# A decoder layer with a gathered expert table: 96 instead of 64 tokens of the second tile by gather, up products of 288 instead of 320 columns

## The chip, the cores and the metric

The kernel runs on one core of one Trainium2 chip. The metric is device time in microseconds (us) of one execution; lower is better. The kernel before has a median of 1505.05 us in 3 runs (1504.67 to 1509.46). One execution was profiled. Every row below is from that execution, and times in rows count from its first instruction.

## The reference, cut to what matters

One decoder layer on 512 tokens of 1024 features: modulation, attention in two head groups, output projection, LayerNorm, and then PEER, an expert layer, followed by the last LayerNorm. The change touches PEER only:

```
q = (hx @ w_pq).reshape(128, 8, 2, 128)                 # per chunk of 128 tokens
sc = einsum('thpd,hpnd->thpn', q, sub_keys)
v_half, i_half = top_k(sc, 16)                           # 16 of 128 keys, two halves
top_s, top_pos = top_k(all 16 x 16 sums, 16)             # 16 of 256 pairs per head
idx = pair of keys -> expert number in 0..16383          # 8 heads x 16 = 128 experts a token
g = softmax(top_s)
a = gelu(einsum('thkd,td->thk', u_tab[idx], hx))         # "up" side
out = einsum('thk,thkd->td', g * a, v_tab[idx])          # "down" side
```

Each token picks 128 of 16384 experts. An expert is one row of 1024 f32 (4 KB) in `u_tab` and one in `v_tab`, 64 MB a table.

## The kernel before, in words

The 512 tokens are four tiles of 128. Up to about 361 us the kernel makes modulation, attention, output projection, LayerNorm and the scores of the keys. Then come two long stages, which the change touches.

**The up stage** (`u_block(e)`, e = 0 to 127, about 361 to 948 us). Block e holds 128 experts. Its 512 KB of `u_T` are loaded (`raw`, three buffers, L98), split by ScalarE into a rounded part `hi` (L90) and by VectorE into the rest `lo` (L91), and multiplied on TensorE with the tokens' features: eight k-slices, three products each (hi by hi, hi by low, low by hi; L114 to L116), so 24 products a block, each of TU columns, one per token. A gelu (L844) gives the activations. Blocks 32 to 111 store them to DRAM (`a_d`) from ScalarE's queue and load them again later (`a_b`); the others stay on chip. TU is 320: the tokens of tiles 2 and 3 and the last 64 of tile 1. This dense path computes every expert for each of its tokens.

**Gathers.** Tile 0 and the first HU = 64 tokens of tile 1 take another way on the up side. For them GpSimd issues indirect DMAs (`fetch`, L771) of 128 rows of `u_tab`, one row per partition, and VectorE multiplies the rows with the tokens' features `h2n` and sums (`dot`, L776). With tile 0 a gather serves one expert of each of 128 tokens, so its up side takes 128 gathers and dots. With 64 tokens a gather serves two experts of each token: the partitions 0 to 63 hold one, 64 to 127 the other, and `h2n` holds the 64 tokens twice. That takes 64 gathers and dots (`gather_part`). Its results go through a gelu, the half in the upper partitions is moved by a small DMA (`far`), and both multiply `g` of tile 1 (L793, L794). Five buffers `gb` hold gathered rows. Tile 0 also takes its down side by gather: 128 gathers of `v_tab`, each added by VectorE into `acc0` (L812).

**make_g.** While the up stage runs, VectorE, ScalarE and TensorE also build for tiles 2, 3 and then 1 the dense table of weights per expert and token (`oh`, `go`, `stage`; L710 to L723; 16 products of 128 columns a step, 48 steps) and write it to DRAM (`g_d`). Tile 1 waits until `gather_part` has set `weighted`. VectorE also runs the top-k of the tiles in the order 1, 2, 3, 0 (`topk`).

**The down stage** (`v_block(n)`, about 948 to 1481 us) multiplies per block of 128 experts the weights times activations with `v_blk`: 18 products of 512 columns for 384 tokens (tiles 1 to 3). The first HU columns of `w` are a copy of the weights (L918, ScalarE), since `g` of these tokens already holds the activations; the other TU are a product with `a` (L920, VectorE).

**Order.** The program interleaves these by generators with costs in us and a rate per block. `pull(gen, us)` advances a generator until the sum of its yields reaches the rate. A dot yields 1.25, an addition to `acc0` 1.2. The rates are RA for gathers before `weighted`, RB after it, RV in the down stage; top-k gets 2.6, 1.2 and at last 0.95 a block; `make_g` gets 0.56 steps a block (GRATE). At down block 116 all gathers that are left are pulled at once. Each engine runs its own instructions in the order fixed in the program, and the DMA queue of SyncE (SP) issues its transfers in order too.

## Time and profile before

| what | value |
|---|---|
| median of 3 runs | 1505.05 us (1504.67 to 1509.46) |
| profiled execution, its own time | 1506.13 us |
| its span, first to last instruction | 1504.4 us |
| mean granted TensorE clock | 0.983 |
| TensorE busy | 1419.4 us (94%) |
| VectorE busy | 1267.4 us (84%) |
| ScalarE busy | 827.4 us (55%) |
| GpSimd busy | 460.2 us (31%) |
| DMA moved | 446.18 MB, mean 297 GB/s |

Engine names in rows: PE is TensorE (PEld its weight loads), DVE VectorE, ACT ScalarE, POOL GpSimd, SP SyncE. Busy time of PE counts from the start of a product to its modelled end, and successive products overlap, so a stretch can show PE fully busy. DMA share is the time that all packets took, divided by 16 engines' time; since packets of one engine may overlap a little, it can pass 1.

### The profile page before, as it was taken

To read this page: it belongs to the slowest core of one execution; us is meant where nothing else is said; L and a number is where in the kernel's file an instruction comes from. 1 tells how busy PE (TensorE), PEld (TensorE's weight loads), DVE (VectorE), ACT (ScalarE), POOL (GpSimd) and SP (SyncE) were. 2 spreads that over 40 slices of the span, in tenths; PEclk is the share of its full clock that TensorE was granted. 3 is DMA by queue.
4 is the path that set the end of the run, shared out by engine and by line. 5 is a ranking of instruction groups with operands and counts; after the bars stand their busy time and mean duration, and the time that the engine had idled before them with its cause. 6 is when DMAs were issued, how large, how long until landed. Compare 5 with 4: busy or idle time off the path is not lost.

```text
span 1504.4 us, 22850 instructions
## 1 busy us (share of the span) xinstructions
PE 1419.4 (94%) x7837; PEld 1247.0 (83%) x7837; DVE 1267.4 (84%) x2602; ACT 827.4 (55%) x1523; POOL 460.2 (31%) x338
## 2 busy tenths in 40 slices
PE   6999988999889999899999999899999999999895
PEld 5777766888779999889999999788888888888684
DVE  6797776799999989779889877799898888997756
ACT  3466633334438998989999943344444444443341
POOL 0000000000254434275455555443443343443100
PEclk9999998999989999999999999999999999999998
DMA  8865453222598899799999999999999999999861
GB/s 301 290 214 165 158 196 133 85 85 71 185 327 290 300 317 348 262 342 411 405 379 403 409 415 395 362 338 347 351 350 368 384 382 384 377 383 391 302 202 56
DMA packets 181526, 446.18 MB, mean 297 GB/s; under 512 B 16609, under 2 KB 87649, under 8 KB 178210
## 3 DMA queue, kind: packets, MB, share of 16 engines
q1 hardware_dynamic: 123810, 263.83, 49.0%
q0 software_dynamic: 46080, 167.79, 29.8%
q10 hardware_dynamic: 11520, 13.11, 2.4%
q8 instruction: 61, 1.00, 0.3%
q14 instruction: 55, 0.45, 0.1%
HBM read 401.38 MB, written 43.26 MB: 296 GB/s over the span
## 4 chain that ended last, share of the span: by engine, by line
PE 59%; DVE 12%; DMA 11%; ACT 8%; issue 7%; POOL 3%; ACTq 0%; SPq 0%; DVEq 0%; POOLq 0%
PE acc L116 10%; PE acc L115 10%; PE acc L114 10%; PE bank L114 5%; PE bank L115 5%; PE bank L116 5%; DMA raw<-u_T 3%; ACT go L716 3%; DVE lo L91 3%; POOL gb L771 3%; PE st L116 3%; PE st L114 3%; PE st L115 3%; PE acc L720 2%; DMA raw<-v_blk 2%
## 5 line engine op out<-in xcount | busy, mean ns | idle before, releaser
L90 ACT CAST hi<-raw 128x1024 fp32r<-128x1024 f32 x288 | 301.7, 1051 | 460.0 <-PE acc L116 217.4
L91 DVE TENSOR_TENSOR lo<-raw,hi 128x1024 fp32r<-128x1024 f32 x288 | 351.6, 1222 | 123.3 <-ACT hi L90 119.7
L116 PE MATMUL st<-h2h,lo 128*128 128x320 f32 x1024 | 319.9, 314 | 14.3 <-DVE lo L91 14.0
L114 PE MATMUL st<-h2h,hi 128*128 128x320 f32 x1024 | 324.1, 317 | 9.6 <-ACT hi L90 9.6
L115 PE MATMUL st<-h2l,hi 128*128 128x320 f32 x1024 | 319.5, 312 | 0.0
L115 PE MATMUL acc<-lo,wh 128*128 128x512 f32 x756 | 295.5, 391 | 5.1 <-DVE lo L91 5.1
L114 PE MATMUL acc<-hi,wh 128*128 128x512 f32 x756 | 295.7, 391 | 3.2 <-ACT wh L928 2.9
L116 PE MATMUL acc<-hi,wl 128*128 128x512 f32 x756 | 296.0, 392 | 0.3 <-DVE wl L929 0.3
L771 POOL DMA_INDIRECT gb<-u_tab,ei x128 | 194.1, 1517 | 188.9 <-DVE gb L776 147.6
L776 DVE SCALAR_TENSOR_TENSOR gb<-gb,h2n 128x1024 f32<-128x1024 f32 x192 | 230.7, 1218 | 20.5 <-DMA gb<-u_tab,ei 15.7
L771 POOL DMA_INDIRECT gb<-v_tab,ei x128 | 158.6, 1239 | 247.6 <-DVE acc L812 225.7
L116 PEld LDWEIGHTS st<-h2h,lo 128*128 128x128 f32 x1024 | 194.4, 190 | 17.6 <-DVE lo L91 17.4
L114 PEld LDWEIGHTS st<-h2h,hi 128*128 128x128 f32 x1024 | 195.1, 190 | 11.9 <-ACT hi L90 11.9
L115 PEld LDWEIGHTS st<-h2l,hi 128*128 128x128 f32 x1024 | 195.0, 190 | 0.0
L771 POOL DMA_INDIRECT gb<-u_tab,eip x64 | 95.8, 1497 | 259.8 <-ACT hi L90 148.8
L716 ACT ACTIVATE go<-oh,iT 128x128 f32<-128x128 bf16 x384 | 168.2, 521 | 8.5 <-DVE oh L710 8.1
L115 PEld LDWEIGHTS acc<-lo,wh 128*128 128x128 f32 x756 | 142.7, 189 | 35.3 <-DVE lo L91 5.5
L114 PEld LDWEIGHTS acc<-hi,wh 128*128 128x128 f32 x756 | 142.8, 189 | 34.0 <-ACT wh L928 3.6
L116 PEld LDWEIGHTS acc<-hi,wl 128*128 128x128 f32 x756 | 142.6, 189 | 31.1 <-DVE wl L929 1.6
L812 DVE SCALAR_TENSOR_TENSOR acc<-gb,w,acc 128x1024 f32<-128x1024 f32 x127 | 162.6, 1281 | 1.0
L122 POOL TENSOR_TENSOR rs_r<-rs_v,mhalf 128x1 f32<-128x1 f32 (+1 forms) x12 | 11.0, 914 | 337.5 <-DVE rs_v L120 301.7
L720 PE MATMUL acc<-go,oh 128*128 128x128 f32 x768 | 108.4, 285 | 4.7 <-ACT go L716 4.7
(220 smaller groups left out, 2001.7 us busy)
## 6 DMA issues: line engine op xcount, KB each, us to landing
raw<-u_T SPq DMA_DIRECT2D x128, 512.0 KB
raw<-v_blk SPq DMA_DIRECT2D x128, 512.0 KB
wada<-w_adaT SPq DMA_DIRECT2D x48, 512.0 KB
g_d<-stage SPq DMA_DIRECT2D x24, 1024.0 KB
gl<-g_d SPq DMA_DIRECT2D x96, 256.0 KB
a_d<-a_s ACTq DMA_DIRECT2D x80, 160.0 KB
a_b<-a_d SPq DMA_DIRECT2D x80, 160.0 KB
raw<-w_pqT SPq DMA_DIRECT2D x16, 512.0 KB
```

What stands on the lines that cost most here:

```text
L90: split.hi = nc.scalar.copy(hi, src)
L91: split.last = nc.vector.tensor_sub(lo, src, hi.bitcast(F32))
L114: nc.tensor.matmul(ps, lh, rh, start=first, stop=False)
L115: nc.tensor.matmul(ps, lh, rl, start=False, stop=False)
L116: nc.tensor.matmul(ps, ll, rh, start=False, stop=last)
L122: nc.gpsimd.tensor_tensor(r, v, mhalf.to_broadcast([P, n]), op=OP.pow)
L716: nc.scalar.activation(go[:, i, :], oh0[:, :, i], AF.Copy, scale=iT[:, 2, t0 + i:t0 + i + 1])
L720: nc.tensor.matmul(ps[:, i * P:(i + 1) * P], oh1[:, 4 * u + i, :], go[:, 4 * u + i, :], start=True, stop=True)
L771: nc.gpsimd.indirect_dma_start(out=b, out_offset=None, in_=A[tab], in_offset=bass.IndirectOffsetOnAxis(ap=idx[:, j:j + 1], axis=0))
L776: paced(nc.vector.scalar_tensor_tensor(b, b, 1.0, h2n, op0=OP.mult, op1=OP.mult, accum_out=acc))
L812: paced(nc.vector.scalar_tensor_tensor(acc0, b, w0[:, j:j + 1], acc0, op0=OP.mult, op1=OP.add))
```

## The change

HU goes from 64 to 96, so TU goes from 320 to 288: 24 x 128 up products lose 32 columns each. `gather_part` becomes two passes. The first serves tokens 0 to 63 with two experts a gather (64 gathers and dots), the second tokens 64 to 95 with four experts a gather (32 gathers and dots; `h2n` holds 32 tokens four times). Each pass loads its list by small DMAs (`eip`, two and four), reloads `h2n` (two and four DMAs), takes its gelu, moves all its results by small DMAs into `far` (two and four), and multiplies `g` once. The rates RA, RV and the last top-k rate change: 1.6 to 2.0, 1.55 to 1.75, 0.95 to 0.8. RB and GRATE stay. The activations that are stored and loaded again have 288 columns instead of 320; the copy of weights in the down stage has 96 columns instead of 64 and the product there 288 instead of 320.

```diff
@@ -38,14 +38,14 @@
 GB = 8
 NS = 80
 GRATE = 0.56
-HU = 64
+HU = 96
 T0U = P + HU
 TU = S - T0U
 LAST = 4
 GBUF = 5
-RA = 1.6
+RA = 2.0
 RB = 1.9
-RV = 1.55
+RV = 1.75
 GP = 6
 AHEAD = 3
 FIN = 24
@@ -777,23 +777,25 @@
 
     def gather_part():
         ei = lists[1]
-        eip = gath.tile([P, HU], I32, name="eip")
-        nc.vector.tensor_copy(eip[0:HU], ei[0:HU, 0:HU])
-        dma(eip[HU:P], ei[0:HU, HU:P])
-        for r in range(2):
-            dma(h2n[r * HU:(r + 1) * HU], h2_d[1][0:HU])
-        dots = gath.tile([P, HU], F32, name="dots1")
-        for j in range(HU):
-            dot(fetch("u_tab", eip, j), dots[:, j:j + 1])
-            yield 1.25
-        nc.scalar.activation(dots, dots, AF.Gelu)
-        far = gath.tile([P, HU], F32, name="far")
-        dma(far[0:HU], dots[HU:P])
         g = best[1][1].rearrange("p h k -> p (h k)")
-        nc.vector.tensor_mul(g[0:HU, 0:HU], g[0:HU, 0:HU], dots[0:HU])
-        nc.vector.tensor_mul(g[0:HU, HU:P], g[0:HU, HU:P], far[0:HU])
+        for r0, n in ((0, 64), (64, 32)):
+            m = P // n
+            eip = gath.tile([P, n], I32, name=f"eip{r0}")
+            for q in range(m):
+                dma(eip[q * n:(q + 1) * n], ei[r0:r0 + n, q * n:(q + 1) * n])
+            for q in range(m):
+                dma(h2n[q * n:(q + 1) * n], h2_d[1][r0:r0 + n])
+            dots = gath.tile([P, n], F32, name=f"dots1{r0}")
+            for j in range(n):
+                dot(fetch("u_tab", eip, j), dots[:, j:j + 1])
+                yield 1.25
+            nc.scalar.activation(dots, dots, AF.Gelu)
+            far = gath.tile([P, P], F32, name="far", tag="far", bufs=1)
+            for q in range(m):
+                dma(far[r0:r0 + n, q * n:(q + 1) * n], dots[q * n:(q + 1) * n])
+            nc.vector.tensor_mul(g[r0:r0 + n], g[r0:r0 + n], far[r0:r0 + n])
+            yield 0.3
         weighted.append(True)
-        yield 0.3
 
     def gather_tile():
         ei = lists[0]
@@ -887,7 +889,7 @@
             g_piece(0, (e - NKEY + 2 * GP + 1) // 2)
         keep(e)
         if e < NB + NS:
-            budget[0] = pull(tk, budget[0] + (2.6 if 1 not in best else 1.2 if 2 not in best else 0.95))
+            budget[0] = pull(tk, budget[0] + (2.6 if 1 not in best else 1.2 if 2 not in best else 0.8))
         if 2 in best and e < NB + NS:
             c1 += GRATE
             while c1 >= 1.0:
```

## Rows read from the trace of the kernel before

**Rows 1.** The page: busy time, then DMA and GB/s in 40 slices.

```profile
PE 1419.4 (94%) x7837; PEld 1247.0 (83%) x7837; DVE 1267.4 (84%) x2602; ACT 827.4 (55%) x1523; POOL 460.2 (31%) x338
...
DMA  8865453222598899799999999999999999999861
GB/s 301 290 214 165 158 196 133 85 85 71 185 327 290 300 317 348 262 342 411 405 379 403 409 415 395 362 338 347 351 350 368 384 382 384 377 383 391 302 202 56
```

**Rows 2.** Windows: us; PE, PEld, DVE, ACT, POOL busy; PEclk; DMA share; GB/s.

```profile
388.70:681.70 293.00, 269.77 (x1783) 257.65 (x1783) 260.98 (x564) 227.52 (x385) 131.83 (x83) 0.97 0.86 306
450.00:600.00 150.00, 145.20 (x989) 138.71 (x988) 141.38 (x323) 133.85 (x231) 61.61 (x40) 1.00 0.88 314
681.70:867.40 185.70, 185.70 (x1358) 185.70 (x1357) 164.36 (x217) 174.11 (x316) 93.67 (x65) 1.00 1.02 402
867.40:947.70 80.30, 79.85 (x546) 79.23 (x546) 61.46 (x87) 32.41 (x48) 44.09 (x32) 1.00 1.03 403
947.70:1145.00 197.30, 193.03 (x848) 158.69 (x847) 174.06 (x228) 81.22 (x145) 81.89 (x64) 0.99 0.98 349
1145.00:1395.00 250.00, 250.00 (x1104) 207.09 (x1103) 218.23 (x257) 102.62 (x180) 96.04 (x78) 1.00 1.05 383
```

**Rows 3.** Timeline, PE, up block without make_g: first product and the next block's first.

```profile
879.72 0.31 PE L114 MATMUL st<-h2h,hi 128*128 128x320 f32 x1
...
883.24 0.31 PE L114 MATMUL st<-h2h,hi 128*128 128x320 f32 x1
```

**Rows 4.** Timeline, PE, down block: a product and the one 18 products later.

```profile
1200.10 0.39 PE L114 MATMUL acc<-hi,wh 128*128 128x512 f32 x1
...
1204.18 0.39 PE L114 MATMUL acc<-hi,wh 128*128 128x512 f32 x1
```

**Rows 5.** Timeline, one make_g step: 16 products of 128 columns on PE.

```profile
702.88 1.95 PE L720 MATMUL acc<-go,oh 128*128 128x128 f32 x16
```

**Rows 6.** The page, DMA queues: packets, MB, share of 16 engines' span.

```profile
q0 software_dynamic: 46080, 167.79, 29.8%
q10 hardware_dynamic: 11520, 13.11, 2.4%
```

**Rows 7.** Groups by line, VectorE, 388.7 to 681.7 us: busy, mean ns | idle before.

```profile
L776 DVE SCALAR_TENSOR_TENSOR gb<-gb,h2n 128x1024 f32<-128x1024 f32 x79 | 95.4, 1216 | 15.2 <-DMA gb<-u_tab,ei 10.9 <-DMA gb<-u_tab,eip 4.2
L91 DVE TENSOR_TENSOR lo<-raw,hi 128x1024 fp32r<-128x1024 f32 x58 | 70.5, 1217 | 7.1 <-ACT hi L90 7.1
```

**Rows 8.** Groups by line, TensorE, 388.7 to 681.7 us.

```profile
L114 PE MATMUL st<-h2h,hi 128*128 128x320 f32 x464 | 148.3, 320 | 9.1 <-ACT hi L90 9.1
L116 PE MATMUL st<-h2h,lo 128*128 128x320 f32 x465 | 146.0, 318 | 9.4 <-DVE lo L91 9.2
```

**Rows 9.** Waits of TensorE, 681.7 to 947.7 us: total, times, longest.

```profile
PE st L116 <- DVE lo L91: 0.3, 1, 0.3
```

**Rows 10.** Timeline of SP's queue where gather_part hands over to tile 0.

```profile
627.54 0.33 SPq L801 DMA_DIRECT2D h2n<-h_d  x1
638.85 0.33 SPq L726 DMA_DIRECT2D g_d<-stage  x1
...
643.33 16.09 SPq L98 DMA_DIRECT2D raw<-u_T  x6
```

**Rows 11.** Waits of SP's queue, whole span: total, times, longest.

```profile
SPq L726 <- ACT dots L789: 11.0, 1, 11.0
```

**Rows 12.** Groups by line, VectorE, 1145 to 1395 us.

```profile
L812 DVE SCALAR_TENSOR_TENSOR acc<-gb,w,acc 128x1024 f32<-128x1024 f32 x78 | 99.9, 1280 | 0.6
L91 DVE TENSOR_TENSOR lo<-raw,hi 128x1024 fp32r<-128x1024 f32 x60 | 73.4, 1223 | 29.9 <-ACT hi L90 28.2 <-issue 1.7
...
L920 DVE TENSOR_TENSOR w<-a_b,gl 128x320 f32<-128x320 f32 x59 | 28.6, 485 | 1.2 <-DMA a_b<-a_d 1.2
```

**Rows 13.** The copy of weights, L918: ns min/median/max, first and last start.

```profile
L918 ACT COPY w<-gl x128: 233/237/243, 947.1 to 1471.0; 128x64 f32<-128x64 f32 x128
```

## The prediction

> **What bounds the kernel now.** I read the page first: TensorE is busy 94% of the span, but its busy time counts modelled ends, so the number to look at is beside it, VectorE at 84%, and the two lines below, where the DMA digits stand at 9 from the middle of the up stage to the end of the gathers [rows 1]. Then the windows by stage [rows 2], since one answer doesn't hold for all of them.
>
> First half of the up stage, blocks 6 to 63 (388.7 to 681.7 us): TensorE needs less than it takes. A block of 24 products of 320 columns runs in 883.24 - 879.72 = 3.52 us, 146.7 ns a product [rows 3], and a make_g step of 16 products takes about 1.7 us (1.95 with the last one's tail, [rows 5]). The stretch has 1393 products of the first kind (those named L114 and L116 are in [rows 8], L115 has as many) and 24 steps: 1393 x 0.1467 + 24 x 1.7 = 204 + 41 = 245 us of 293. VectorE is busy 261 of 293, and in the middle of it 141.4 of 150, 94% [rows 2]; TensorE's waits that are seen are for what ScalarE and VectorE split [rows 8]. VectorE is the tightest here; DMA has room (share 0.86).
>
> Second half, blocks 64 to 127 (681.7 to 947.7): TensorE has no gap to speak of, 0.3 us of wait in 266 [rows 9], and DMA is full too: share 1.02 and 1.03, 402 and 403 GB/s [rows 2]. Two bounds lie on each other.
>
> Down stage: 18 products of 512 columns take 4.08 us, 226.7 ns each [rows 4], and TensorE is busy 250.00 of 250; the DMA share is 0.98 to 1145 us, then 1.05 at 383 GB/s with smaller packets [rows 2].
>
> **The products.** From 512 to 320 columns the pitch falls by 80 ns, 0.417 ns a column. So 288 columns give 133.3 ns, still above the 112 ns or so (1.95 us less some 0.27 of the last one's own, over 15) that products of 128 columns need [rows 5], and 32 columns are 13.3 ns: 3072 x 13.3 = 41.0 us of TensorE's work. By stretch: blocks 0 to 5 about 2 us, to block 63 18.6 us, after it 20.5 us (62.8 blocks or so at 0.32). The granted clock is 1.00 in nearly all windows, the upper level, 2.4 GHz [rows 2].
>
> The Trainium skill gives less: TensorE: Matmul & The Clock Gate, section Back-to-back issue gap, has a sustained spacing of 81 ns at 128 columns and 131 ns at 512, an estimate of 4.2 ns for 32 columns and 13 us in all. The 226.7 and 146.7 ns of this trace disagree with it, and the measurement decides.
>
> **The gathers.** I count them by the yields. The list of tile 1 is known at block 6. Before, 64 dots at 1.6 / 1.25 a block fill blocks 6 to 55, then 1.9 / 1.25 = 1.52 a block; in the down stage 1.55 / 1.25 and 1.55 / 1.2. After: 96 at 2.0 / 1.25 = 1.6 fill blocks 6 to 65, then 1.52, then 1.75 / 1.25 and 1.75 / 1.2 = 1.46. Up to block 63 that is 76 before (the trace has 79, [rows 7]) and 93 after; blocks 64 to 127 98 and 97; down stage 146 and 162, ending at down block 112 and 111. So 17 more in the first half, 1 less in the second, 16 more in the down stage. The weights of tile 1 are ready at block 66 instead of 55; make_g needs them at block 78, so nothing waits. Top-k of tile 0 ends at block 63 instead of 56, before the list is needed at 66.
>
> One gather is 29.8% x 1504.4 / 320 = 1.40 us of all DMA engines (0.52 MB); a store of activations 2.4% x 1504.4 / 80 = 0.45 us [rows 6], and a tenth of it, 0.045 us, falls away; I take the same for loading them. On VectorE one dot is 1.22 us [rows 7], one addition 1.28 [rows 12].
>
> **First half.** DMA: 293 x 0.86 + 17 x 1.40 = 276 us, still under 293 x 1.05. VectorE: 261 + 17 x 1.22 = 282 us. If TensorE set this stage, it would fall by 18.6 us. If VectorE sets it, at the occupancy of its own stretch (261 / 293 = 0.89) it becomes 282 / 0.89 = 316, +23; at the 0.943 of the 150 us in its middle 299, +6. The nearest row is that one, as rates are more even after the change and the gap between the lists goes; TensorE's relief shortens some of the waits for split buffers. I take +3, ends -18.6 and +23.
>
> The second pass adds a hand-over: SP stood between 627.5 and 638.9 us, 11.0 us of it behind the gelu of the dots, and then sent six loads at once [rows 10, 11]. Loads queued behind it feed blocks three ahead, some 15 us at 5 us a block, so most of a second stand of this kind is hidden; dots that need the reloaded `h2n` wait in VectorE's queue and the splits behind them. Bounds 0 and 11; I take +1, nearer to the lead that the buffers give.
>
> **Second half.** TensorE's work falls by 20.5 us, but DMA time is 185.7 x 1.02 + 80.3 x 1.03 = 272.1 us of share, less one gather (1.4) and 48 stores (2.1): 268.6. At today's share that is 3 us gained; at the 1.05 that the down stage holds it is 256, 10 us gained. Ends -20.5 and -3; I take -11, nearest to the 1.05.
>
> **Down stage.** TensorE's work doesn't change. Up to 1145 us the share time is 193.4 + 7.7 x 1.40 = 204, at 1.05 194 of 197.3: hidden. After it 262.5 + 8.3 x 1.40 - 61 x 0.045 = 271.4, at 1.05 258.5: 8 us over 250. Since TensorE never waits there now, 1.05 isn't shown to be the limit: ends 0 and +8, I take +4, the middle. VectorE gets 10 more additions (13 us) and loses a tenth of the 485 ns product over 61 blocks (3 us, [rows 12]): 228 of 250, not the bound. The wider copy costs ScalarE at most half of its 237 ns a block [rows 13]; it is busy 103 of 250, so nothing. The other small DMAs and the wider rows for LayerNorm's output are hidden in the same way.
>
> **The sum.** +3 + 1 - 11 + 4 = -3 us; blocks 0 to 5 give 0, as VectorE fills them with top-k. Against the profiled execution: span 1504.4 - 3 = 1501.4, and 1.7 us lie around the span (1506.13 - 1504.4). The median is 1.1 under that execution, so 1502 us. Some 41 us leave TensorE, and nearly all is refused by DMA and VectorE.
>
> **Rivals.** A, DMA has room: its share follows what is asked for, and TensorE's order set the pace. For it: 402 GB/s isn't the most that the page shows (415 in one slice, [rows 1]). Against: three stretches with different demands all stand at 1.02 to 1.05. The second half then gives -20, the first -3, the down stage 0: 1482. The Trainium skill speaks for it: HBM Reference, section Specifications, has about 425 GB/s for a core that streams alone; an estimate by it is 106 MB in 249 us where 266 are taken, 17 us gained. No run here shows 425.
>
> B, slower: VectorE's fixed order in blocks 6 to 65. Every dot stands ahead of the next split in its queue; if the occupancy stays at 0.89, the first half costs +23, and with -10 and +4 for the rest that is 1522. It decides at an occupancy of 0.93: above it the second half pays for the first. For it: 15.2 us of VectorE's waits are for gathered rows [rows 7], and there are more of them. Against: 0.943 over 150 us.
>
> C, the products don't get shorter, as the weight load sets their pitch: nothing from TensorE, and DMA work still grows: +6 + 1 - 3 + 4, about 1513. Against it stand the two pitches that differ by columns, and the 112 ns.
>
> **How the numbers follow.** The case of the sum has 0.48, its own range 1493 to 1511; A 0.23; B 0.26; C 0.03. A measurement of this kernel can tell about 0.3%, 4.5 us, from no change. The sum's case lies 3 us under, so of its 0.48 I give 0.19 to faster, 0.19 to the same and 0.10 to slower. With A, B and C: faster 0.42, same 0.19, slower 0.39; rounded 0.42, 0.20 and 0.38. The range reaches to A and a little beyond B's, 1482 to 1523.
>
> **What would show it.** Pitch of up products: 133 ns. A block without make_g: 3.20 us where TensorE doesn't wait. First half: VectorE over 0.94 busy and TensorE's waits for `lo` grown. Second half: DMA share over 1.03, and TensorE with waits that it doesn't have now; if it has none and the stretch is 20 us shorter, A is right. After 1145 us of today: TensorE under 250 of 250. If the first half is over 10 us longer, B is right. The prediction is wrong in its core if DMA share rises over 1.08 or the down stage gets shorter.

## The result, and the profile after

The changed kernel takes 1545.22 us (median of 4 runs, 1541.22 to 1550.94), the kernel before beside it 1506.54 (4 runs): a ratio of 1.0259 [1.0231, 1.0287]. It is 39 us slower, where 3 us faster was forecast, and lies outside the range. The profiled execution took 1546.69 us, its span 1544.9.

The page after, in the lines of [rows 1] and [rows 6]: busy time by engine; DMA share and GB/s in 40 slices; queues with packets, MB and share.

```profile
PE 1414.7 (92%) x7837; PEld 1229.5 (80%) x7837; DVE 1298.9 (84%) x2665; ACT 828.9 (54%) x1524; POOL 512.8 (33%) x370
...
DMA  8856353222698898889999999999999999999962
GB/s 309 288 187 194 121 197 126 83 84 68 235 320 297 317 328 303 313 326 322 401 385 412 382 410 397 373 341 385 372 367 384 386 383 383 385 383 389 310 222 73
...
q0 software_dynamic: 50688, 184.57, 32.1%
q10 hardware_dynamic: 11520, 11.80, 2.2%
```

TensorE is busy only 4.7 us less (1419.4 before) although 3072 products lost 32 columns each, and VectorE's 84% now lies over a longer span. Where the time went is seen by stage, cut at the first product of up blocks 0, 6, 64 and 107 and the first split of `wl`, the low part of the weights, in down blocks 0, 48 and 112. The windows of the changed kernel, columns as in [rows 2]: blocks 6 to 63, the middle of them, 64 to 106, 107 to 127, down blocks 0 to 47, 48 to 111.

```profile
392.80:711.80 319.00, 268.88 (x1785) 254.21 (x1783) 276.79 (x593) 225.80 (x378) 141.20 (x98) 0.91 0.86 305
480.00:600.00 120.00, 104.27 (x728) 97.80 (x726) 108.12 (x215) 96.78 (x169) 56.13 (x36) 0.97 0.89 317
711.80:906.70 194.90, 186.33 (x1420) 183.36 (x1421) 169.85 (x226) 179.43 (x328) 96.97 (x66) 0.99 1.01 390
906.70:989.20 82.50, 70.66 (x508) 67.77 (x506) 64.47 (x90) 31.72 (x49) 52.99 (x34) 1.00 1.03 398
989.20:1184.60 195.40, 192.79 (x839) 158.09 (x838) 177.73 (x247) 82.15 (x144) 91.63 (x70) 0.99 1.01 367
1184.60:1465.60 281.00, 271.84 (x1166) 219.55 (x1166) 244.22 (x293) 111.92 (x194) 119.27 (x86) 0.99 1.03 376
```

The kernel before at the same marks from block 64 on:

```profile
681.70:876.20 194.50, 194.50 (x1421) 194.50 (x1420) 170.51 (x226) 178.81 (x322) 98.16 (x69) 1.00 1.02 402
876.20:953.80 77.60, 75.46 (x508) 74.16 (x506) 61.41 (x85) 29.75 (x45) 44.81 (x30) 1.00 1.02 393
953.80:1148.80 195.00, 192.42 (x839) 158.11 (x838) 170.97 (x222) 80.89 (x144) 77.64 (x62) 0.99 0.98 350
1148.80:1420.20 271.40, 266.30 (x1167) 219.67 (x1166) 233.53 (x277) 110.60 (x194) 96.15 (x77) 0.99 1.03 377
```

| stretch | before | after | difference | forecast |
|---|---|---|---|---|
| ahead of block 0 | 361.0 | 365.7 | +4.7 | 0 |
| blocks 0 to 5 | 27.7 | 27.1 | -0.6 | 0 |
| blocks 6 to 63 | 293.0 | 319.0 | +26.0 | +3 and +1 |
| blocks 64 to 127 | 272.1 | 277.4 | +5.3 | -11 |
| down block 0 to the end | 550.6 | 555.7 | +5.1 | +4 |

The differences sum to 40.5 us, that of the spans. The first row is no effect: in kernels that don't differ there it was 359.9 to 368.1 us. Each stage is read from one execution, and repeats of the same order give its spread. Blocks 6 to 63 took 319.0 us here and 313.2 in a kernel that differs only later (the one with fewer late gathers, below). In six kernels with the same order there, blocks 64 to 127 took 271.0 to 280.6 us and blocks 64 to 106 188.0 to 197.1. Differences inside these carry nothing below. The repeat of blocks 6 to 63:

```profile
393.30:706.50 313.20, 265.09 (x1784) 250.98 (x1782) 275.47 (x589) 225.35 (x378) 142.94 (x98) 0.92 0.86 311
```

Of the second half, blocks 64 to 106 kept their time, and blocks 107 to 127 took 82.5 us instead of 77.6. GpSimd issued 34 gathers there instead of 30 (the count behind POOL's time), and the time goes with them: 81.0 to 84.4 us in the six kernels, with 32 to 34 gathers, and 76.0 with 27 in the one with fewer late.

The products did get shorter. Timeline of PE: the first product shown and one 24 products later, then a make_g step as in [rows 5].

```profile
884.89 0.29 PE L114 MATMUL st<-h2h,hi 128*128 128x288 f32 x1
...
888.09 0.29 PE L114 MATMUL st<-h2h,hi 128*128 128x288 f32 x1
...
888.49 1.95 PE L720 MATMUL acc<-go,oh 128*128 128x128 f32 x16
```

3.20 us for 24 products is 133.3 ns each, as forecast. For 32 columns fewer, the sustained spacings in the Trainium skill (TensorE: Matmul & The Clock Gate, section Back-to-back issue gap) would give an estimate of 4.2 ns; the two traces show 146.7 - 133.3 = 13.4, and the measurement decides.

What hid that relief in blocks 6 to 63: groups of VectorE by line, to set against [rows 7], then waits (total, times, longest) of ScalarE, TensorE and SP's queue.

```profile
L776 DVE SCALAR_TENSOR_TENSOR gb<-gb,h2n 128x1024 f32<-128x1024 f32 x93 | 112.0, 1219 | 8.5 <-DMA gb<-u_tab,eip 8.5
L91 DVE TENSOR_TENSOR lo<-raw,hi 128x1024 fp32r<-128x1024 f32 x58 | 70.9, 1223 | 14.4 <-ACT hi L90 14.2
...
ACT hi L90 <- DMA raw<-u_T: 31.8, 18, 5.8
...
PE st L114 <- ACT hi L90: 25.2, 21, 2.4
...
SPq L98 <- DVE lo L91: 134.5, 27, 13.4
SPq L726 <- ACT stage L723: 44.3, 8, 11.1
```

ScalarE's wait for `raw` in the kernel before, blocks 6 to 63:

```profile
ACT hi L90 <- DMA raw<-u_T: 29.2, 16, 5.4
```

VectorE's work grew by 15.8 us (261.0 to 276.8), but the stretch by 26. VectorE's occupancy (its busy share of the stretch) fell from 0.891 to 0.868; in the middle, 480 to 600 us, it was 108.12 of 120, 0.90. Its longest wait is now for `hi`, 14.2 us (7.1 before), and `hi` waits for `raw`: loads of `u_T` come late. But ScalarE waited for `raw` nearly as long before, 29.2 us against 31.8. So the loads aren't later in sum than they were; what they cost is what the experiments ask.

### The profile page after: what moved, and what is told of

Its sections match the earlier page's. It is cut to its first block, busy times and chain, and to the rows that moved or that the text cites. A ratio compares the mean times of both kernels' runs of the same rounds, so it can differ in the third digit from the quotient of the medians.

```text
span 1544.9 us, 23012 instructions
## 1 busy us (share of the span) xinstructions
PE 1414.7 (92%) x7837; PEld 1229.5 (80%) x7837; DVE 1298.9 (84%) x2665; ACT 828.9 (54%) x1524; POOL 512.8 (33%) x370
## 4 chain that ended last, share of the span: by engine, by line
PE 28%; issue 20%; DVE 16%; DMA 15%; POOL 11%; ACT 9%; SPq 0%; POOLq 0%; DVEq 0%; ACTq 0%
POOL gb L771 10%; DMA raw<-u_T 6%; DVE lo L91 4%; PE bank L114 4%; PE bank L116 4%; PE bank L115 4%; ACT go L716 4%; DVE gb L776 3%; ACT hi L90 2%; PE st L116 2%; PE acc L115 2%; PE acc L116 2%; PE acc L114 2%; PE st L114 2%; DMA gl<-g_d 2%
## 5 line engine op out<-in xcount | busy, mean ns | idle before, releaser
L114 PE MATMUL st<-h2h,hi 128*128 128x288 f32 x1024 | 317.7, 310 | 30.9 <-ACT hi L90 30.8
L116 PE MATMUL st<-h2h,lo 128*128 128x288 f32 x1024 | 312.7, 308 | 22.1 <-DVE lo L91 21.9
L115 PE MATMUL st<-h2l,hi 128*128 128x288 f32 x1024 | 310.8, 304 | 0.0
L776 DVE SCALAR_TENSOR_TENSOR gb<-gb,h2n 128x1024 f32<-128x1024 f32 x224 | 269.1, 1220 | 19.5 <-DMA gb<-u_tab,eip 8.5
L771 POOL DMA_INDIRECT gb<-u_tab,ei x128 | 187.5, 1465 | 179.3 <-DVE gb L776 165.3
L771 POOL DMA_INDIRECT gb<-u_tab,eip x96 | 138.1, 1438 | 306.1 <-DMA eip<-ei 149.9
L771 POOL DMA_INDIRECT gb<-v_tab,ei x128 | 175.6, 1372 | 190.8 <-DVE acc L814 169.8
L114 PEld LDWEIGHTS st<-h2h,hi 128*128 128x128 f32 x1024 | 200.4, 196 | 37.8 <-ACT hi L90 37.6
L116 PEld LDWEIGHTS st<-h2h,lo 128*128 128x128 f32 x1024 | 199.3, 195 | 27.2 <-DVE lo L91 27.1
L720 PE MATMUL acc<-go,oh 128*128 128x128 f32 x768 | 116.0, 294 | 21.9 <-ACT go L716 21.8
L720 PEld LDWEIGHTS acc<-go,oh 128*128 128x128 f32 x768 | 103.1, 201 | 30.8 <-ACT go L716 26.7
```

Source lines behind the costliest of these rows:

```text
L114: nc.tensor.matmul(ps, lh, rh, start=first, stop=False)
L115: nc.tensor.matmul(ps, lh, rl, start=False, stop=False)
L116: nc.tensor.matmul(ps, ll, rh, start=False, stop=last)
L720: nc.tensor.matmul(ps[:, i * P:(i + 1) * P], oh1[:, 4 * u + i, :], go[:, 4 * u + i, :], start=True, stop=True)
L771: nc.gpsimd.indirect_dma_start(out=b, out_offset=None, in_=A[tab], in_offset=bass.IndirectOffsetOnAxis(ap=idx[:, j:j + 1], axis=0))
L776: paced(nc.vector.scalar_tensor_tensor(b, b, 1.0, h2n, op0=OP.mult, op1=OP.mult, accum_out=acc))
```

## The experiments

Theories, as the expectations name them:

- V: VectorE's work and its density set the first half (blocks 6 to 63).
- H: the second hand-over does, where one pass's dots end and the next list and features are loaded.
- C: TensorE's lower clock does. The granted clock is 0.91 there, 0.97 before; between its levels of 1.2 and 2.4 GHz that is (1 - 0.91) / 0.5 x 319 = 57 us at the lower one.
- D1: the gathers' transfers set the first half.
- D2: DMA's limit holds the second half (blocks 64 to 127) and the down stage.
- Later W: VectorE's fixed order is held up by late data; Q: SP's order makes them late; S: ScalarE sets blocks 64 to 106.

Each result is a median, its ratio to the kernel before run beside it, and in brackets the ratio's 95% interval. Windows and waits are of one execution each.

### Rates and passes

The kernel before with the new rates:

```diff
-RA = 1.6
+RA = 2.0
-RV = 1.55
+RV = 1.75
-... else 0.95))
+... else 0.8))
```

> The kernel before (64 tokens, products of 320 columns) with the changed kernel's three rates: RA 2.0, RV 1.75, last top-k rate 0.8. Gathers stay 320 but come earlier. Theory V (VectorE and the gathers' density in the first half of the up stage set its length): the first half takes 10 to 15 us more than before's 293 us, since 15 or so gathers move into it, and the whole is 0 to 10 us slower than before. Theory H (the second hand-over and its reloads cost the first half): no second hand-over here, so first half within 4 us of before. Theory C (TensorE's gaps drop its clock to 1.2 GHz, and that makes the stage long): half-clock time between 361 us and block 64 follows the gaps; near before's 20 us if the gaps don't grow.

The changed kernel with two old rates:

```diff
-RA = 2.0
+RA = 1.6
-... else 0.8))
+... else 0.95))
```

> The changed kernel with RA 1.6 and the last top-k rate 0.95 of the kernel before; RV stays 1.75, so that all gathers end before down block 116. The first half of the up stage then has as many gathers as before (about 76), the rest comes later. Theory V: its excess of 25 us falls to under 8, and the down stage gains a few us in return; whole 1525 to 1535. Theory H: the hand-over stays, so 10 us or more of the excess stay. Theory C: half-clock time falls with the gaps, from 58 us towards 25.

The changed kernel without its second pass (the up side of tokens 64 to 95 is left out):

```diff
-        for r0, n in ((0, 64), (64, 32)):
+        for r0, n in ((0, 64),):
```

> The changed kernel without the second pass: the up side of tokens 64 to 95 is left out (no gathers, dots, hand-over for them), the products keep 288 columns and the rates stay. Theory V and H alike: most of the 39 us go, whole 1495 to 1510; V says that the first half is no shorter than 293 - 5 us since 80 gathers still lie there, H says it falls by 12 us or more against the changed kernel's 317. If the products' 41 us arrive in full, the whole is near 1470, which neither expects: DMA holds the second half.

Measured: 1513.7 us, 1.0030 [1.0005, 1.0055]; 1544.5, 1.0223 [1.0180, 1.0265]; 1514.55, 1.0044 [1.0021, 1.0068]. Their windows of blocks 6 to 63, in this order:

```profile
388.80:683.80 295.00, 268.11 (x1784) 259.80 (x1783) 252.59 (x544) 226.23 (x384) 106.72 (x74) 0.96 0.81 289
...
389.70:687.30 297.60, 259.68 (x1785) 248.67 (x1784) 256.97 (x555) 226.62 (x382) 118.09 (x80) 0.93 0.84 298
...
390.00:685.70 295.70, 257.08 (x1784) 245.05 (x1783) 251.37 (x545) 225.53 (x383) 100.95 (x72) 0.95 0.80 284
```

The count behind POOL's time is that of the gathers: 74, 80 and 72 give 295 to 298 us, and the width of the products makes no difference (74 at 320 columns, 72 at 288). The first run missed what it was made for: some 15 gathers more were expected in the stretch, and there were 9 fewer (74 against 83), since those of tile 0 wait for its list and began only at block 57. As a whole stretch it therefore tests V little. The third doesn't tell V from H; its time is a little over the 1495 to 1510 of both.

H falls by place. The changed kernel's second hand-over begins with the gelu of the second pass:

```profile
720.26 0.23 ACT L792 ACTIVATE dots<-dots 128x32 f32<-128x32 f32 x1
```

That is in block 65, behind the stretch that ends at 711.8 us; with the old rates it comes at 753.2 us. So blocks 6 to 63 hold one hand-over in every one of these kernels, as before. Blocks 64 to 106, where the second lies, took 194.9 us after and 194.5 before.

The old rates bring the first half to 297.6 us, but don't save the change: the whole stays at 1544.5, where V had 1525 to 1535. What the first half leaves is gathered later, to 1489.3 us instead of 1432.3, and the end of the down stage (from down block 112) takes 96.1 us instead of 79.3.

Blocks 8 to 47 alone show the density: 195 us before, 198 with the old rate and both passes, but 210 with the new rate at either width, and 214 after. The first run against the kernel before, both with 320 columns, has 64 instead of 55 dots there. VectorE's busy time rises by 7 us (182.5 to 189.5), and the time by 15.

### TensorE's clock

Six more products a block in blocks 6 to 65 of the changed kernel, into the block's own bank, which its first real product clears:

```diff
+        for _ in range(FILL if 6 <= e < 66 else 0):
+            nc.tensor.matmul(ps, h2h[:, 0, 0:P], h2h[:, 0, T0U:], start=True, stop=True)
```

> The changed kernel with six extra products of 288 columns on resident operands ahead of each of the up blocks 6 to 65, written into the block's own bank before its first product clears it: 0.8 us a block that TensorE does while it waits. Theory C: half-clock time in the first half falls from 58 us to under 20 and the whole gets 10 to 18 us faster than the changed kernel. Theories V and H: the clock is a consequence; the half-clock time may fall, but the whole stays within 5 us of the changed kernel, or gets slower by the 48 us of extra products where they aren't covered.

1535.6 us, 1.0164 [1.0119, 1.0210]. The window of blocks 6 to 63:

```profile
389.20:707.70 318.50, 293.01 (x2127) 285.02 (x2126) 284.94 (x601) 231.15 (x392) 145.97 (x101) 0.96 0.87 314
```

The clock rose from 0.91 to 0.96 and the stretch kept its 319 us. The added products are a second change in this run, 58 x 6 x 133.3 ns = 46 us of work, so it doesn't show what a higher clock alone would bring. It shows that the granted clock rose when TensorE's waits were filled, and that the stretch takes up this much more of TensorE's work without growing: TensorE doesn't set its length.

The whole is some 10 us faster than the changed kernel, the lower end of what C had (10 to 18) and more than the 5 of V and H. But the gain isn't in the stretch that C explains. Of the 12 us between the profiled executions, 6.9 lie in blocks 64 to 106 (188.0 instead of 194.9) and 4.6 ahead of block 0, where nothing differs. Why the whole is faster stays open.

### Dots and gathers apart

The changed kernel without the 96 gathers of tile 1 (left out, and GpSimd's issuing of them with it; the dots read one tile that is loaded once), and with the gathers but dots of 32 columns (the other 992 are left out):

```diff
-                dot(fetch("u_tab", eip, j), dots[:, j:j + 1])
+                dot(still, dots[:, j:j + 1])                     # the first
+                b = fetch("u_tab", eip, j)                       # the second
+                ...scalar_tensor_tensor(b[:, 0:32], b[:, 0:32], 1.0, h2n[:, 0:32], ...)
```

> The changed kernel with the 96 gathers of tile 1 left out, their 96 dots kept on a tile that stays in place: VectorE's work as in the changed kernel, without the gathers' DMA and their waits. Theory V (VectorE's own work at a given density sets the first half of the up stage, 319 us from block 6 to 64 in the changed kernel, 293 before): it stays over 305, and blocks 8 to 48 over 205 (214 in the changed kernel, 195 before). Theory D1 (the gathers' transfers and the waits for them set it): it falls under 295, blocks 8 to 48 under 195.

> The changed kernel with its 96 gathers of tile 1 kept and their dots cut to 32 of 1024 columns, so that VectorE does some 0.1 instead of 1.2 us for each: some 100 us of VectorE's work leave blocks 6 to 65, DMA and GpSimd do the same. Theory V: the first half falls under 280 us, blocks 8 to 48 under 185. Theory D1: it stays over 305.

1520.72 us, 1.0106 [1.0074, 1.0139], and 1497.48 us, 0.9931 [0.9913, 0.9949]. Window and two waits of the first, then the window of the second:

```profile
390.50:683.30 292.80, 257.19 (x1785) 240.72 (x1783) 274.40 (x589) 224.28 (x378) 2.43 (x2) 0.97 0.48 161
...
ACT hi L90 <- DMA raw<-u_T: 6.5, 5, 2.4
...
DVE lo L91 <- ACT hi L90: 3.5, 3, 1.9
```

```profile
391.20:665.70 274.50, 247.87 (x1785) 240.10 (x1784) 190.63 (x602) 222.62 (x383) 122.19 (x101) 0.96 0.95 356
```

Neither V nor D1 holds alone: the first run is under the 295 us that D1 named, the second under the 280 that V named. Without most of the dots' work (VectorE 86 us less busy) the stretch falls by 45 us, 39 from the repeat of 313.2, with all its gathers and a DMA share of 0.95. Without the gathers it falls by 26, or 20, with VectorE's work nearly unchanged (274.4, occupancy 0.937). There VectorE's idle time fell from 42.2 to 18.4 us; 10.7 of that is its wait for `hi`, 8.5 that for gathered rows. Theory W joins the two.

### Fewer gathers late, and another rate in the down stage

The changed kernel with fewer gathers in the second half, and the kernel before with more early in the down stage:

```diff
-RB = 1.9
+RB = 1.5
-RV = 1.75
+RV = 2.0
```

```diff
-        c2 = pull(gt, c2 + RV)
+        c2 = pull(gt, c2 + (1.75 if n < 48 else RV))
```

> The changed kernel with RB 1.5 instead of 1.9 and RV 2.0 instead of 1.75: after block 66 some 1.2 instead of 1.5 gathers a block, the rest moved to the down stage. Theory D2 (DMA at its limit kept the narrower products from shortening blocks 64 to 107, which take 194.9 us after the change and 194.5 before): without 14 or so gathers of 1.4 us they take 180 to 185 us, what products and make_g need (43 x 3.2 + 24 x 1.78 = 180). If something else holds them (VectorE's order, ScalarE), they stay within 4 us of 194. The down stage gets 15 to 25 us longer under D2, at a DMA share of 1.05; the whole is then no faster than the changed kernel.

> The kernel before (64 tokens) with RV 1.75 in down blocks 0 to 47, which load no stored activations, and 1.55 after: 8 gathers move into blocks with DMA room, and the gathers end near block 106 instead of 112. Theory D2: blocks 0 to 47 stay at 195 us, since the share rises from 0.98 to under 1.05, and blocks 104 to 111, which take 41.7 us before as the last gathers meet the seven loads for the end, lose 4 to 10 us: whole 1498 to 1503. If that stall has another cause, the whole stays at 1505 to 1509.

1552.8 us, 1.0311 [1.0287, 1.0335], and 1499.32 us, 0.9968 [0.9947, 0.9989]. The first in blocks 64 to 106, the second in down blocks 48 to 111:

```profile
706.50:899.00 192.50, 185.55 (x1420) 181.88 (x1421) 156.58 (x200) 180.02 (x330) 72.75 (x54) 1.00 0.99 364
```

```profile
1148.70:1409.90 261.20, 261.20 (x1154) 216.28 (x1153) 229.41 (x280) 109.46 (x192) 85.83 (x70) 1.00 1.04 377
```

With 12 gathers fewer, blocks 64 to 106 stay at 192.5 instead of the 180 to 185 that D2 has: D2 isn't enough there. In blocks 107 to 127 fewer gathers (27 instead of 34) do give time, 82.5 to 76.0, and the down stage takes it back, as D2 had it (down blocks 48 to 111: 293.7). In the other kernel the gathers end at 1363 us, ahead of the loads at the down stage's end; down blocks 104 to 111 fall from 41.7 us to 31.9, the stretch by 10, of which the end gives 3 back.

### Late loads

The changed kernel with a fourth buffer for the loads of `u_T`, and with a sixth for gathered rows:

```diff
     def u_split(e):
+        if e >= 6 and e % 4 == 3:
+            raw = gath.tile([P, KB, P], F32, name="raw_4", tag="raw_4", bufs=1)
+            queue.append(dma(raw, A["u_T"][e]))
+            return split(raw, [P, KB, P])
```

```diff
-GBUF = 5
+GBUF = 6
```

> The changed kernel with a fourth buffer for the loads of u_T (blocks 7, 11, 15 and so on), so that SP's queue can send a load one block earlier; work and order on VectorE are the same. In blocks 6 to 63 the changed kernel takes 319 us with VectorE busy 277; without the gathers' transfers 293 with VectorE busy 274, and the idle time that goes is its waits for hi (14.2 to 3.5) and for gathered rows (8.5 to 0). Theory W (the fixed order on VectorE is held up by data that come late, u_T's loads above all): VectorE's wait for hi falls under 6 us and the first half to 303-311 us. Theory V (the number of VectorE instructions by itself): 317-321. Theory B2 (the bytes of gathers and loads share the DMA engines and nothing helps but fewer of them): no change within 4 us, and the wait for raw stays at 25-32 us on ScalarE. Second half and down stage: the same within 4 us in all.

> The changed kernel with six instead of five buffers for gathered rows; GpSimd can issue a gather one dot earlier. Theory W: VectorE's wait for gathered rows falls from 8.5 us to under 3, and the first half by 4 to 9 us (310-315 of 319), if the earlier gathers don't push the loads of u_T back; if they do, ScalarE's wait for raw grows over 32 us and the first half stays within 3 us. Theory V: 317-321. Down stage: gathers there are taken from the same buffers, its time stays within 3 us since DMA is at its limit.

1527.46 us, 1.0119 [1.0083, 1.0156], and 1545.0 us, 1.0235 [1.0215, 1.0255]. The first's window and its longest wait of ScalarE, then the second's window:

```profile
392.50:695.80 303.30, 261.08 (x1783) 245.70 (x1783) 276.18 (x592) 225.23 (x378) 143.32 (x98) 0.94 0.89 321
...
ACT hi L90 <- PE st L115: 61.4, 21, 13.4
```

```profile
395.20:709.70 314.50, 262.63 (x1785) 247.79 (x1783) 276.25 (x593) 226.46 (x378) 143.94 (x99) 0.94 0.86 311
```

The load buffer takes 16 us off (10 from the lower repeat of 313.2), and ScalarE no longer waits for `raw` at all; VectorE's wait for `hi` falls to 6.6 us, just over the 6 expected. The whole's ratio falls from 1.0259 to 1.0119, with intervals that lie apart. VectorE's work is the same (276.2), so part of the stretch was time lost to late loads. A sixth buffer for gathered rows leaves their wait at 8.0 us, the stretch between its two repeats and the whole time as it was. So W holds for the loads, not for the gathered rows.

The fourth buffer in the kernel before, on top of the rate of 1.75: its memory once from the gathered rows, once from activations kept on chip (24 blocks instead of 32).

```diff
-GBUF = 5
+GBUF = 4
```

```diff
-NB = 32
+NB = 24
-NS = 80
+NS = 88
```

> The kernel before with the rate 1.75 in down blocks 0 to 47 (the version that took 1499 us), and a fourth buffer for u_T's loads, its memory taken from the gathered rows (four buffers instead of five). A fourth buffer took 16 us from the first half of the changed kernel (319.0 to 303.3). Theory W (a load of u_T waits until VectorE, behind its dots, has read the buffer; so VectorE's queue sets when the next data come): the kernel before has the same loop, with VectorE's idle time 32 us of 293 there, so its first half falls by 5 to 12 us to 278-285 and the whole to 1487-1495. If the loop bites only at the denser rate: first half 287-293, whole 1497-1501. If four buffers of gathered rows are too few: VectorE's wait for them grows over 25 us in the first half (15.2 before), and it takes 295 or more.

> As the one before it, but with five buffers for gathered rows; the memory comes from keeping the activations of 24 instead of 32 blocks on chip, so 88 instead of 80 are stored and loaded again. That adds 8 stores and 8 loads at 0.45 us of all DMA engines, 3.6 us each way, the stores in blocks 24 to 31 of the up stage, where DMA has room, the loads in the down stage, which stands at its limit. Theory W: first half 278-285 as above, and the down stage up to 4 us longer: whole 1488-1497. If the loop bites only at the denser rate: first half 287-293, whole 1498-1504.

1504.06 us, 0.9972 [0.9952, 0.9992], and 1495.44 us, 0.9918 [0.9889, 0.9947]. The second's window of blocks 6 to 63 and its waits for gathered rows and loads:

```profile
391.50:679.30 287.80, 268.42 (x1785) 256.67 (x1784) 258.26 (x562) 224.94 (x382) 133.55 (x82) 0.97 0.86 313
...
DVE gb L780 <- DMA gb<-u_tab,ei: 12.0, 5, 5.1
...
ACT hi L90 <- DMA raw<-u_T: 2.3, 1, 2.3
```

Here too ScalarE's wait for `raw` is nearly gone (29.2 us before), but the first half stays near the 289.5 that it took without the fourth buffer. So at the old rate late loads cost little, as one expectation had it. With the fourth buffer in both kernels, the first half is 303.3 and 287.8 us, 15.5 apart, no more than VectorE's work (276.2 and 258.3). With four buffers for gathered rows it took 286.0, and blocks 64 to 127 took 11 us more than without the edit (284 instead of 273); the whole missed the 1497 to 1501 expected.

The version with 24 blocks on chip is the fastest of this study: 0.8% faster than the kernel before. Its median lies in the 1488 to 1497 that W named, though its first half doesn't. The profiled execution was the slowest of its six (1499.67 us), so no trace shows where the rest of the gain lies.

### Two bounds in blocks 64 to 106

In that window of the changed kernel ScalarE is busy 179.4 us of 194.9, and it issues 42 stores of activations at 0.33 us, 14 us, that don't count as busy. Its groups by line:

```profile
L716 ACT ACTIVATE go<-oh,iT 128x128 f32<-128x128 bf16 x192 | 84.3, 535 | 0.3 <-DVE oh L710 0.2
L723 ACT COPY stage<-acc 128x512 f32<-128x512 f32 x47 | 47.4, 1112 | 0.4 <-ACT a_s L846 0.4
L90 ACT CAST hi<-raw 128x1024 fp32r<-128x1024 f32 x44 | 46.0, 1055 | 14.7 <-DMA raw<-u_T 9.0 <-DVE gb L776 2.7 <-PE acc L720 2.4
L846 ACT ACTIVATE a_s<-st 128x288 f32<-128x288 f32 x42 | 17.3, 413 | 0.0
```

The changed kernel with most of the copy to `stage` left out (16 of 128 rows are copied), and the same with the rates RB 1.5 and RV 2.0:

```diff
-  nc.scalar.copy(stage[:, :, w:w + 4]..., ps...)
+  nc.scalar.copy(stage[:, 0:16, w:w + 4]..., ps...[:, :, 0:16])
```

> The changed kernel in which ScalarE copies only 16 of 128 rows of the dense table of weights from each of make_g's two banks (the two stage tiles are set to zero once instead; the rest of the table is left out, and the same bytes are written to DRAM). That takes about 0.85 of 47 x 1.11 us, some 43 us of ScalarE's work, out of blocks 64 to 107; TensorE's, VectorE's and DMA's work stay. Theory S (ScalarE sets these blocks: 179 us busy and 14 us of issuing stores in 195): they fall to 180-189 us, TensorE's own 43 x 3.20 + 24 x 1.7 = 179 being the floor, or 188 if DMA's share tops out at 1.05 (194.9 x 1.012 / 1.05). Theory D2 (DMA's limit alone): 193-197. First half: within 6 us of 319, since ScalarE isn't full there (226 of 319); if it falls by more than 10, ScalarE's queue sits in VectorE's loop too.

> As the one before it, with the rates RB 1.5 and RV 2.0 (about 12 gathers fewer in blocks 64 to 107, as in the kernel with fewer late gathers, where these blocks took 192.5 us with ScalarE's whole work). Theory S with TensorE behind it: 178-184 us. Theory S with DMA behind it: the kernel with the short copies alone takes about 188 and this one 179-183. If neither ScalarE nor DMA sets these blocks: both stay at 190-197. Down stage longer than with 1.75, as in that kernel (293.7 instead of 281.0 for down blocks 48 to 111).

1541.34 us, 1.0225 [1.0202, 1.0248], and 1540.25 us, 1.0209 [1.0188, 1.0229]. Windows of blocks 64 to 106, with ScalarE's wait for `raw`, of the one and of the other:

```profile
702.80:898.70 195.90, 189.17 (x1421) 183.24 (x1420) 170.20 (x227) 146.03 (x326) 98.90 (x69) 1.00 1.01 391
...
ACT hi L90 <- DMA raw<-u_T: 30.8, 14, 6.0
```

```profile
709.70:895.80 186.10, 183.71 (x1422) 182.67 (x1421) 158.44 (x204) 147.03 (x329) 79.47 (x57) 0.99 1.01 390
...
ACT hi L90 <- DMA raw<-u_T: 10.6, 7, 2.9
```

| us in blocks 64 to 106; 64 to 127 | rates RB 1.9, RV 1.75 | RB 1.5, RV 2.0 |
|---|---|---|
| ScalarE's whole work | 194.9; 277.4 | 192.5; 268.5 |
| short copies | 195.9; 278.1 | 186.0; 257.4 |

Only with both taken away do blocks 64 to 106 fall clearly, to 186.0, just over the 178 to 184 expected, with TensorE busy 183.7 (its own work is 43 x 3.20 + 24 x 1.7 = 178). The whole second half falls by 20 us against the changed kernel, and by 15 against the kernel before (272.1), where TensorE's relief is 20.5. Short copies alone give nothing, fewer gathers alone 9 us, 6.5 of it behind block 106, where make_g has ended. So S alone and D2 alone both fall, and the four kernels fit two bounds near 195 us at once, ScalarE and DMA.

Each cell is one execution, and the kernel with added products took 188.0 in blocks 64 to 106 with the changed kernel's order; the 186.0 by itself is therefore weak. Firmer are the 257.4 for the second half, 11 us under 268.5 by the short copies, and the medians: short copies move the ratio from 1.0259 to 1.0225, inside the intervals, but from 1.0311 to 1.0209 where late gathers are fewer too.

With ScalarE relieved alone, DMA's share still stops at 1.01, and ScalarE waits 30.8 us for `raw`. So DMA's limit here reads as 1.01 to 1.02 and not the 1.05 of the down stage.

### SP's order

A piece of the first half of the changed kernel: VectorE's split that frees a load buffer, ScalarE's copies, and SP's queue.

```profile
505.63 1.23 DVE L91 TENSOR_TENSOR lo<-raw,hi 128x1024 fp32r<-128x1024 f32 x1
...
508.33 1.99 ACT L723 COPY stage<-acc 128x512 f32<-128x512 f32 x2
...
510.35 0.33 SPq L726 DMA_DIRECT2D g_d<-stage  x1
510.77 10.05 SPq L98 DMA_DIRECT2D raw<-u_T  x4
```

The buffer is free at 506.86 us (505.63 + 1.23), but the load goes out at 510.77: a store of make_g stands ahead of it and waits for ScalarE's copies to 510.32. The stores moved to ScalarE's queue, in the changed kernel and in the fastest version:

```diff
-                    queued(dma(*held.pop()))
+                    nc.scalar.dma_start(*held.pop())
```

> The changed kernel with the stores of make_g's stage (24 in all) issued from ScalarE's queue instead of SP's, so no load of u_T stands behind a store that waits for ScalarE's copies. Theory Q (SP's order holds the loads back): the first half falls by 8 to 16 us, from 319 to 303-311, ScalarE's wait for raw from 31.8 to under 15, nearly what the fourth buffer gave. Theory W in its first form (VectorE's lo behind the dots holds them back): 316-321, and SP's waits for lo take the place of those for stage. Blocks 64 to 107: ScalarE gets 12 issues of 0.33 us, 4 us, where it is full: 194.9 to 199, unless the loads freed there give it back.

> The fastest version so far (320 columns, fourth buffer for loads of u_T, 24 blocks' activations kept on chip, rate 1.75 in down blocks 0 to 47; 1495 us) with the same stores from ScalarE's queue. Theory Q: first half 280-286 instead of 287.7, blocks 64 to 107 195-199 for ScalarE's added issues, whole 1490-1497. Theory W: first half 286-290, whole 1495-1501.

1545.05 us, 1.0259 [1.0204, 1.0313], and 1504.97 us, 0.9984 [0.9960, 1.0008]. The changed kernel's blocks 6 to 63 and 64 to 106 with this edit, and the waits of ScalarE for `raw` and of SP for `lo` in the first:

```profile
389.30:698.70 309.40, 263.27 (x1785) 251.48 (x1784) 281.10 (x597) 227.01 (x382) 144.93 (x99) 0.92 0.87 316
698.70:902.60 203.90, 190.62 (x1420) 187.14 (x1420) 166.80 (x220) 181.75 (x328) 97.00 (x66) 0.97 0.98 374
...
ACT hi L90 <- DMA raw<-u_T: 11.1, 8, 2.7
...
SPq L98 <- DVE lo L91: 183.7, 35, 13.6
```

The wait for `raw` falls from 31.8 to 11.1 us, and the first half to 309.4: 10 us, or 4 against the lower repeat. That is Q's range, but W's sign came too: SP's waits for `lo` grow from 134.5 to 183.7 us, so with the store gone the load stands behind VectorE's splits. SP's order is a part of the lateness, less than the fourth buffer took away.

In blocks 64 to 106, where ScalarE is full, its 12 added issues are 4 us, and the time is 203.9 us: 9 over the changed kernel, 7 over the slowest repeat. Nothing is left of the gain. The fastest version loses by the edit, outside the ranges of Q and W; its first half took 291.8 us. The Trainium skill (Trainium Kernel Development and Optimization, section Key Constraints) says that issuing DMAs from several engines only saves issue time. Here, in one execution each, the choice of queue also moved 4 to 10 us in one stage and 7 to 9 in the next, by what stands behind the waiting store and by how full its new engine is.

## Why the prediction was wrong

**First half: +3 and +1 against +26 (+20 in the repeat).** The step that failed is "I take +3". It took VectorE's occupancy as 0.943, that of 150 us in the middle of the stretch, so that the added dots would mostly fill VectorE's idle time, and argued that more even rates and TensorE's relief would shorten its waits. The dots came as counted (93 in blocks 6 to 63), but occupancy fell, to 0.868 and 0.88 in two executions and to 0.90 in the middle. VectorE's added work, 15.8 us, arrived in full, and some 10 us of lost time (6 in the repeat) came on top. Its "VectorE over 0.94 busy" didn't come, and TensorE's waits grew for `hi` (9.1 to 25.2 us), not for `lo`.

Behind the lost time is a loop that the prediction had no term for. A load of `u_T` can go out only when VectorE has read the buffer, and that split stands behind more dots; then the load stands in SP's queue behind a store; then it shares DMA with more gathers; and the next splits wait for it. Taking away the dots' work (-39 to -45 us), the gathers (-20 to -26) or the buffer limit (-10 to -16) each shortens the stage. What remains with four buffers, 303.3 against 293.0, goes with 15.2 us more of VectorE's work.

Rival B, with a chance of 0.26, is nearly what happened here: dots ahead of splits, its +23 between the two executions, its occupancy of 0.89 a little over theirs, and the prediction's own sign for it, a first half over 10 us longer. Its total of 1522 fell short, as it too counted on 10 us from the second half. The +1 for the hand-over stood in the wrong stage: by the prediction's own count the second pass ends at block 65, and there it did.

**Second half: -11 against +5.3.** The step that failed is taking "the 1.05 that the down stage holds" for these blocks: the share stays at 1.01 in blocks 64 to 106 and at 1.03 behind them, where it was 1.03 already [rows 2]. Of the 3 us at today's share nothing was left either, since 34 instead of 30 gathers fell into blocks 107 to 127, 5.6 us of DMA at 1.40 each, where the time grew by 4.9. And a bound was overlooked that [rows 2] shows: ScalarE busy 174.11 of 185.70 us, besides its store issues. The prediction weighed TensorE and DMA there and never priced ScalarE. (Its 62.8 blocks at 0.32 us should be 64, which give its 20.5 us.) Before the change three engines stood within a few per cent of each other in blocks 64 to 106: TensorE's own work 43 x 3.52 + 24 x 1.7 = 192 of 194.5 us, ScalarE 178.8 and some 14 of issuing stores, DMA's share 1.02. So shortening one could bring next to nothing.

**Down stage: +4 against +5.1.** The sum is right, in part by luck. Down blocks 48 to 111 took 9.6 us more, over the upper end of +8 named for the stretch, and the end, which the prediction didn't price, 4.8 less. Between down blocks 48 and 96 the share is 1.04 to 1.05, at 378 to 386 GB/s, in every kernel here, while down blocks 48 to 111 took 261 to 294 us with the number of gathers there; so that limit, which the prediction left open, is one.

**What held:** the pitch of 133 ns; nearly the count of gathers (15 more in the first half, 17 forecast); that the second half refuses TensorE's relief, there by DMA and, as far as shown, ScalarE together. Rivals A and C are excluded by the share and the pitch. What stays open: how much of the loop is VectorE's order, how much SP's and how much DMA's, since one execution of the first half varies by 6 us; and whether the fastest version's first half has one bound or several.

## What to carry to other kernels

Before a bound is relieved in a stage, read the busy time of every engine in that stage's window and add the DMA issues that don't count as busy: one at 92% beside the bound can take the gain. An instruction added to an engine that also frees load buffers can cost more than its own duration (here 7 us of work cost 15 in blocks 8 to 47); ask what its queue frees, and which store stands ahead of the next load. An occupancy read in the best part of a stage isn't what added work will meet in all of it. A share that DMA reaches in one stage isn't its limit in another with another mix of transfers. And before a cost is put into a stage, check by the program's own count that it falls there.

## What the runs showed of the hardware

DMA's share of busy time tops out at different levels in two stages of the same kernel. In blocks 64 to 106 it is 1.01 to 1.02, at 386 to 404 GB/s, in 15 of the 18 kernels and 0.98 to 0.99 in the other three; between down blocks 48 and 96 it is 1.04 to 1.05, at 378 to 386 GB/s, in all. TensorE's granted clock went with its waits: 0.91 in the first half of the changed kernel, 0.97 without the gathers' transfers, 0.96 with added products and no change in the stretch's time.
